# Attention scores on one core: the kernel moved into one critical section with its own semaphores, and one weight load for two products

## The chip, the core and the metric

One NeuronCore of a Trainium2 chip runs the kernel. The metric is the device time of one execution in microseconds (us), lower is better. Where I speak of a trace, it is of one execution, profiled; where I speak of a median, it is of 3 to 11 executions. PSUM is the memory that TensorE writes its products to, an eviction is the copy out of it, a store is the transfer of one head's result to memory, and a transfer lands when it reports itself done (each of the 16 DMA engines reports for its share).

## The reference

```python
def setup_inputs():
    batch, n_heads, seq, head_dim = 8, 12, 1024, 64
    return {"q": randn(batch, n_heads, seq, head_dim).astype(float32) * 0.1,
            "k": randn(batch, n_heads, seq, head_dim).astype(float32) * 0.1}

def reference(q, k):
    return np.einsum('bhid,bhjd->bhij', q, k).astype(np.float32)
```

There are 96 heads. Each takes two inputs of 1024x64 floats and gives 1024x1024 floats: 50.33 MB are read and 402.65 MB written. A head's result is 4.194 MB.

## The kernel before

The heads are worked in blocks of 2G heads, with G = 1, 1, 2, and then 4 eleven times. So block 0 is heads 0 and 1, block 1 heads 2 and 3, block 2 heads 4 to 7, block 3 heads 8 to 15, and so on. For each block the inputs are loaded, cast to half precision on GpSimd, transposed so that the head dimension lies on the partitions, multiplied on TensorE, copied out of PSUM by ScalarE and stored. A framework of tile pools places the semaphores.

```python
sizes = [1, 1, 2] + [GMAX] * (BH // (2 * GMAX) - 1)
PE_BLOCKS = 2                      # blocks 0 and 1 are transposed by TensorE
in_pool   = tile_pool(bufs=3)      # float32 inputs
half_pool = tile_pool(bufs=3)      # half-precision parts, two to a block
tr_pool   = tile_pool(bufs=2)      # transposed q and k of a block
out_pool  = tile_pool(bufs=3)      # one head's result, 32 KB a partition
po_pool   = tile_pool(bufs=2, space=PSUM)

def transpose_rows(self, x):       # blocks 0 and 1
    for t in range(NT):
        nc.tensor.transpose(t_ps[:, t], self.halves[x][:, t], ident)
    nc.vector.tensor_copy(out=dst, in_=src)

def transpose_quads(self, part, x):  # all others, 32x32 blocks
    nc.vector.transpose(out=dst, in_=src)

def scores(self, n, side):
    for u in range(NT // 2):
        for tt in range(2):
            for j in range(2):
                nc.tensor.matmul(ps[:, tt, js], qT[cs, g, 2*u + tt], kT[cs, g, js])
        nc.scalar.copy(out=dst, in_=ps)      # head 0: half of it on VectorE
        for do in side.get(u, []): do()      # transposes of the next block, loads
    nc.sync.dma_start(out=of[self.first + n]..., in_=o_sb...)
# ... (the first output buffer holds the inputs of blocks 0 to 2 at the start)
```

## Time and profile before

| | before |
|---|---|
| median of 3, first rounds | 1064.69 us (1064.45 to 1066.07) |
| traced execution | 1067.61 us, span 1065.8 |
| bytes moved | 453.26 MB |
| mean rate over the span | 425 GB/s |
| busiest compute engine | TensorE, 66% |

The DMA engines are full from 2 us to 1055 us, and no compute engine comes near to its limit.

### The profile page before, as it was taken

To read this page: it belongs to the slowest core of one execution; us is meant where nothing else is said; L and a number is where in the kernel's file an instruction comes from. 1 tells how busy PE (TensorE), PEld (TensorE's weight loads), DVE (VectorE), ACT (ScalarE), POOL (GpSimd) and SP (SyncE) were. 2 spreads that over 40 slices of the span, in tenths; PEclk is the share of its full clock that TensorE was granted. 3 is DMA by queue.
4 is the path that set the end of the run, shared out by engine and by line. 5 is a ranking of instruction groups with operands and counts; after the bars stand their busy time and mean duration, and the time that the engine had idled before them with its cause. 6 is when DMAs were issued, how large, how long until landed. Compare 5 with 4: busy or idle time off the path is not lost.

```text
span 1065.8 us, 4231 instructions
## 1 busy us (share of the span) xinstructions
PE 700.8 (66%) x1568; PEld 240.7 (23%) x1568; DVE 428.6 (40%) x57; ACT 694.3 (65%) x384; POOL 354.0 (33%) x206
## 2 busy tenths in 40 slices
PE   6686756756765675675675667567567667777770
PEld 2232212212222221221222222122122222222220
DVE  4768922900940670290094067029109406700000
ACT  2687657656765765666675677576667657777771
POOL 7769055036206505502620650550261064000000
DMA  9999999999999999999999999999999999999997
GB/s 384 440 430 434 421 427 439 427 429 427 434 422 433 433 431 421 435 427 424 434 433 413 433 431 418 422 434 423 426 432 432 428 430 432 432 433 433 432 430 313
DMA packets 21909, 453.26 MB, mean 425 GB/s; under 512 B 2432, under 2 KB 2432, under 8 KB 3968
## 3 DMA queue, kind: packets, MB, share of 16 engines
q1 hardware_dynamic: 14976, 406.85, 89.2%
q10 hardware_dynamic: 6912, 46.14, 10.4%
q8 instruction: 12, 0.20, 0.1%
q14 instruction: 9, 0.07, 0.0%
HBM read 50.33 MB, written 402.65 MB: 425 GB/s over the span
## 4 chain that ended last, share of the span: by engine, by line
DMA 70%; ACT 17%; PE 7%; DVE 1%; POOL 1%; issue 1%; ACTq 0%; SPq 0%; POOLq 0%
DMA out_dram<-o_sb 70%; ACT o_sb L166 17%; PE ps L155 7%; POOL half_sb L111 1%; DVE kT L128 0%; DMA early<-in_q_dram 0%; DVE o_sb L162 0%; DVE kT L139 0%; DVE o_sb L164 0%; PE ps L136 0%; ACT o_sb L161 0%; DVE qT L139 0%; ACTq L166 0%; POOL half_sb L93 0%; SPq L74 0%
## 5 line engine op out<-in xcount | busy, mean ns | idle before, releaser
L155 PE MATMUL ps<-kT,qT 64*128 64x512 f16 x1536 | 696.9, 617 | 333.6 <-ACT o_sb L166 328.2
L166 ACT COPY o_sb<-ps 128x2048 f32<-128x2048 f32 x379 | 689.0, 1868 | 335.5 <-DMA out_dram<-o_sb 302.2
L111 POOL CAST half_sb<-x_sb 32x2048 f16<-32x2048 f32 x176 | 332.1, 1887 | 531.6 <-DMA x_sb<-in_k_dram 507.1
L155 PEld LDWEIGHTS <-qT 64*128 64x128 f16 x1536 | 237.4, 157 | 791.2 <-issue 788.3
L128 DVE STREAM_TRANSPOSE qT<-half_sb 128x2048 f16<-128x2048 f16 (+1 forms) x24 | 214.2, 8926 | 477.8 <-POOL half_sb L111 477.8
L128 DVE STREAM_TRANSPOSE kT<-half_sb 128x2048 f16<-128x2048 f16 (+1 forms) x24 | 216.2, 9009 | 0.0
L111 POOL CAST half_sb<-early 32x1024 f16<-32x1024 f32 x16 | 16.5, 1033 | 2.6 <-DMA early<-in_k_dram 1.9
L136 PE MATMUL ps<-ident,half_sb 128*128 128x128 f16 x32 | 3.9, 309 | 6.7 <-POOL half_sb L93 6.2
L161 ACT COPY o_sb<-ps 128x1024 f32<-128x1024 f32 x4 | 4.0, 1012 | 5.5 <-PE ps L155 5.5
L162 DVE COPY o_sb<-ps 128x1024 f32<-128x1024 f32 x4 | 4.9, 1224 | 5.2 <-ACT o_sb L161 5.2
L161 ACT ACT_TABLE_LOAD x1 | 1.3, 1283 | 7.7 <-DMA early<-in_k_dram 7.7
L93 POOL CAST half_sb<-early 128x512 f16<-128x512 f32 x8 | 4.7, 613 | 3.4 <-DMA early<-in_q_dram 3.2
L139 DVE COPY qT<-ps 128x1024 f16<-128x1024 f16 x2 | 2.4, 1219 | 7.3 <-PE ps L136 7.3
L136 PEld LDWEIGHTS <-half_sb 128*128 128x128 f16 x32 | 3.3, 142 | 8.3 <-POOL half_sb L93 6.2
L139 DVE COPY kT<-ps 128x1024 f16<-128x1024 f16 x2 | 2.4, 1218 | 3.8 <-PE ps L136 3.8
L164 DVE COPY o_sb<-ps 128x2048 f32<-128x2048 f32 x1 | 2.3, 2292 | 2.0 <-PE ps L155 2.0
masks.py:199 POOL TENSOR_SCALAR_AFFINE_SELECT ident<-ident 128x128 f16<-128x128 f16 x1 | 0.3, 292 | 0.1
masks.py:197 POOL MEMSET ident<- 128x128 f16 x1 | 0.2, 204 | 0.3 <-POOLq L275 0.3
L275 POOL MEMSET const-float32-0.0<- 128x1 f32 x1 | 0.1, 98 | 0.2 <-issue 0.2
L275 POOL MEMSET const-bfloat16-1.0<- 128x1 bf16 x1 | 0.1, 100 | 0.0
L275 POOL MEMSET const-uint8-127<- 128x1 uint8 x1 | 0.1, 100 | 0.0
L275 POOL MEMSET const-float32-1.0<- 128x1 f32 x1 | 0.1, 98 | 0.0
## 6 DMA issues: line engine op xcount, KB each, us to landing
out_dram<-o_sb SPq DMA_DIRECT2D x96, 4096.0 KB, 23.2
x_sb<-in_k_dram ACTq DMA_DIRECT2D x22, 1024.0 KB, 29.6
x_sb<-in_q_dram ACTq DMA_DIRECT2D x20, 1024.0 KB, 18.6
x_sb<-in_q_dram SPq DMA_DIRECT2D x2, 1024.0 KB, 13.0
early<-in_k_dram ACTq DMA_DIRECT2D x4, 256.0 KB, 5.1
early<-in_q_dram SPq DMA_DIRECT2D x4, 256.0 KB, 4.7
early<-in_q_dram SPq DMA_DIRECT2D x2, 512.0 KB, 7.2
early<-in_k_dram ACTq DMA_DIRECT2D x2, 512.0 KB, 7.6
```

The source lines that it names most:

```text
L93: nc.gpsimd.tensor_copy(out=self.halves[x][:, :, half], in_=self.raw[half][:, x].rearrange("p (r d) -> p r d", d=D),)
L111: nc.gpsimd.tensor_copy(out=dst[:, :, b % 2], in_=raw[32 * b : 32 * b + 32, :, :, h],)
L128: pin(nc.vector.transpose(out=dst, in_=src))
L136: pin(nc.tensor.transpose(t_ps[:, t], self.halves[x][:, t], ident))
L139: pin(nc.vector.tensor_copy(out=dst, in_=src))
L155: nc.tensor.matmul(ps[:, tt, js], qT[cs, g, 2 * u + tt], kT[cs, g, js])
L161: pin(nc.scalar.copy(out=dst[:, 0], in_=ps[:, 0]))
L162: pin(nc.vector.tensor_copy(out=dst[:, 1], in_=ps[:, 1]))
L164: pin(nc.vector.tensor_copy(out=dst, in_=ps))
L166: pin(nc.scalar.copy(out=dst, in_=ps))
L275: nc = _bacc.Bacc("TRN2", target_bir_lowering=False, num_devices=1)
```

## The change

The intent is to spare the framework's waits and instructions. Everything stands in one critical section, each engine's order is written out by hand, and 18 semaphores replace the framework's. Two products that use the same q weights share one weight load. Along with it more changes: blocks 0 and 1 are now transposed by VectorE too, block 0's casts are shared out over three engines, head 1's evictions all go to ScalarE, some early loads are issued at other heads, and VectorE's order is fixed. The half-precision parts rotate through three buffers as before, but blocks 0 and 1 now take two each. The core of the diff, cut:

```diff
-    PE_BLOCKS = 2
-    half_pool = ctx.enter_context(tc.tile_pool(name="half_pool", bufs=3))
+    parts = [sb([P, 2 * GMAX * NT * D], F16, f"part{i}") for i in range(3)]
+        b.parts = [parts[(2 * i + p) % 3][:, : 2 * b.elems] for p in range(2)]
 ...
-                pin(nc.tensor.transpose(t_ps[:, t], self.halves[x][:, t], ident))
 ...
+    def pool_casts(b):
+        for half in range(2):
+            if half == 0:
+                if b.i == 1:
+                    nc.gpsimd.wait_ge(s_tr, 2)
+                elif b.i > 1:
+                    nc.gpsimd.wait_ge(s_tr, 4 * (b.i - 1) + 2)
+            nc.gpsimd.wait_ge(*b.loaded[half])
+            for dst, src in casts(b, half):
+                nc.gpsimd.tensor_copy(out=dst, in_=src).then_inc(s_cast, 1)
 ...
+                a = nc.tensor.matmul(o[:, t, :512], w, kT[cs, g, :512])
+                a = same_weights(a.ins, o[:, t, 512:], w, kT[cs, g, 512:])
 ...
+    with tc.tile_critical():
 ...
+        for n in range(4):
+            load(*stream.pop(0), (nc.sync, nc.scalar)[n % 2])
 ...
+        transposes(blocks[0])
+        for h in range(BH):
+            copies(h)      # head 2 waits for the last cast of block 2
+            store(h)
+            if h == 0:
+                for b in blocks[1:]:
+                    transposes(b)
```

## The prediction

> **What bounds the kernel now.** I read the page first: its slices, its chain of waits, its groups. Then the windows, the groups kept apart by form, and the timelines of the first 135 us.
>
> From the page (40 slices of 26.6 us; DMA is the mean busy share of the 16 DMA engines in tenths) and its chain:
>
> ```profile
> DMA  9999999999999999999999999999999999999997
> GB/s 384 440 430 434 421 427 439 427 429 427 434 422 433 433 431 421 435 427 424 434 433 413 433 431 418 422 434 423 426 432 432 428 430 432 432 433 433 432 430 313
> DMA 70%; ACT 17%; PE 7%; DVE 1%; POOL 1%; issue 1%; ACTq 0%; SPq 0%; POOLq 0%
> ```
>
> The DMA engines are full in every slice but the last; no compute engine passes 66%. The reader should see that there is no free time to win in the middle: 453.26 MB (402.65 of them the result) have to pass, and they pass at about 430 GB/s from the start.
>
> The windows (us, busy us and count by engine, granted clock, DMA share, GB/s) show how little is lost at the ends:
>
> ```profile
> 0.00:26.00 26.00, 15.53 (x53) 7.01 (x54) 10.67 (x8) 7.22 (x7) 19.51 (x28) 1.00 0.98 391
> 26.00:50.00 24.00, 17.17 (x44) 5.97 (x43) 18.77 (x5) 14.51 (x8) 16.78 (x11) 1.00 1.00 428
> 50.00:100.00 50.00, 38.05 (x84) 12.91 (x84) 36.31 (x4) 40.00 (x22) 38.42 (x21) 1.00 1.00 430
> 100.00:135.00 35.00, 23.70 (x53) 8.02 (x52) 31.07 (x4) 21.82 (x12) 7.59 (x5) 1.00 1.01 431
> 135.00:1000.00 865.00, 575.15 (x1268) 196.41 (x1268) 331.74 (x37) 577.82 (x318) 271.69 (x144) 1.00 1.00 429
> 1055.00:1066.00 11.00, 0.00 (x0) 0.00 (x0) 0.00 (x0) 0.00 (x0) 0.00 (x0) 1.00 0.31 135
> ```
>
> At the start only about 2.5 us are lost (26 us at 391 instead of 430). In the last 11 us the DMA engines end one after the other: the trace's landings of the last stores lie 8.6 us apart between the first and the last of the 16 engines, against 0.3 us for the first store and 1.8 us at 130 us. So some engines are slower, and the slowest sets the end. So the only thing a change of waits and instructions can do is to keep the DMA engines fed sooner, or to let them starve. It is the start that has to be followed, and for it I need durations:
>
> ```profile
> L166 ACT COPY o_sb<-ps 128x2048 f32<-128x2048 f32 x379 | 689.0, 1868 | 335.5 <-DMA out_dram<-o_sb 302.2 <-PE ps L155 25.4 <-POOL half_sb L111 7.6
> L128 DVE STREAM_TRANSPOSE qT<-half_sb 128x1024 f16<-128x1024 f16 x2 | 9.3, 4635 | 0.0
> L93 POOL CAST half_sb<-early 128x512 f16<-128x512 f32 x8 | 4.7, 613 | 3.4 <-DMA early<-in_q_dram 3.2
> L161 ACT COPY o_sb<-ps 128x1024 f32<-128x1024 f32 x4 | 4.0, 1012 | 5.5 <-PE ps L155 5.5
> L161 ACT ACT_TABLE_LOAD x1 | 1.3, 1283 | 7.7 <-DMA early<-in_k_dram 7.7
> ```
> ```profile
> 11.31 17.20 POOL L111 CAST half_sb<-early 32x1024 f16<-32x1024 f32 x16 [1.95 <-DMA early<-in_k_dram]
> 39.18 30.89 POOL L111 CAST half_sb<-x_sb 32x2048 f16<-32x2048 f32 x16 [6.40 <-DVE kT L128]
> 62.34 9.23 DVE L128 STREAM_TRANSPOSE qT<-half_sb 128x2048 f16<-128x2048 f16 x1 [14.63 <-POOL half_sb L111]
> 89.14 9.52 DVE L128 STREAM_TRANSPOSE kT<-half_sb 128x2048 f16<-128x2048 f16 x1
> 9.69 3.56 PE L155 MATMUL ps<-kT,qT 64*128 64x512 f16 x8 [1.59 <-DVE kT L139]
> 19.80 10.17 SPq L170 DMA_DIRECT2D out_dram<-o_sb  x2
> ```
>
> In these timelines (start, length, what): the 16 casts of block 2 take 17.2 us, of a block of four 30.9; four large transposes run from 62.34 to 98.66, so 36.3 us; the first product is at 9.69 and the first store at 19.80, while the loads still fill the DMA engines.
>
> **What the Trainium skill says.** "DMA: Bandwidth & Descriptors", section "Where 436 GB/s comes from", gives 435.2 GB/s as the ceiling of the path to SBUF; the trace agrees (429 to 433 when full). "TensorE: Matmul & The Clock Gate", section "Architectural detail: the array is 16× 32×32, not 1× 128×128", says TensorE can pull a weight load ahead of matmuls in flight; here matmuls with a 157 ns load between each start 0.43 us apart, which is that same page's cold gap of N/1.2 for N = 512 (section "Back-to-back issue gap"), so the load is hidden already. "VectorE: DVE Perf Modes", section "The three transpose paths", has the vector transpose at 32x32 blocks only, TensorE's whole; here eight TensorE transposes took 1.05 us and a 1.22 us copy, where a 128x1024 vector transpose takes 4.6.
>
> **The change, part by part.**
> (1) Shared weights: 768 of 1536 weight loads go. They are hidden, TensorE waits 328 us for evictions, and the DMA engines set the end: 0 us.
> (2) Own semaphores: fewer waits on the issuing queues. Loads are no longer held for a landing, but they already saturate the DMA engines: 0, at most 1 us.
> (3) Blocks 0 and 1 lose the TensorE transposes and go by vector transposes. Block 0: its loads land as before, 4.4 us (first half) and 5.7 us (second; block 0's last cast input). ScalarE issues 8 loads of 0.43 us from 0.73, to 4.2, loads its table to 5.5, then does 6 of the 16 casts. 512 columns by the line through 1.012 and 1.868 us are 0.58, say 0.6: to 9.1. VectorE (6) and GpSimd (4 of about 0.6) are done sooner. Four transposes of 512 columns: the step between starts is 4.33 us for 1024 and 8.93 for 2048, so about 2.15: to 17.8. Head 0: 16 matmuls at 0.43 and the last copy (VectorE, 1.22, now beside ScalarE's rather than after it) 8.3: first store at 26.1 instead of 19.8.
> (4) VectorE's order is now fixed: block 0, head 0's copies, then blocks 1, 2, 3. GpSimd's casts of block i+1 wait for the first two of block i's four transposes, as three part buffers serve two blocks. So the start is one serial chain: 26.1; first two transposes of block 1, 4.4: 30.5; casts of block 2, 17.2: 47.7; first two transposes of block 2, 9.1 (39.18 less 30.08): 56.8; casts of block 3, 30.9: 87.7; its transposes, 36.3: 124.0; head 8's first products 1.9 and four copies 7.5: store 8 is issued at 133.4. A first DMA flows about 1.5 us after its issue (windows of 2 us: 17 GB/s to 2 us, 315 after): 134.9.
> Before that store the DMA engines can only be given the loads of blocks 0 to 4 (12.58 MB) and 8 stores of 4.194 MB: 46.1 MB. The kernel before has moved 26x391 + 24x428 + 50x430 + 34.9x431 = 57.0 MB by then. The 10.9 MB short cost 10.9/0.429 = 25.3 us. As cross-check, the gaps: loads (8.39 MB) end at 22.5, store 0 flows at 27.6: 5 us. Stores 0 and 1 end near 47; store 2 has its copies held by the casts of block 2 (its buffer holds the early inputs) to 47.7, plus 7.6 and 1.5: 10 us. Stores 2 to 7 and four loads, 29.4 MB, fill 56.8 to 125; store 8 flows at 134.9: 10 us. The sum is 25. The slow DMA engines are behind by 1.8 us and use part of the gap: 25.3 - 1.8 = 23.5. After head 8, a block needs 30.9 of casts and 36.3 of transposes in some 88 us of DMA: hidden.
> Sum: 1064.7 + 23.5 = 1088.2.
>
> **Rivals.**
> A. The start is fed well enough and the DMA engines hide all: 1063 to 1066. For: the chain of before also has casts and transposes at the start, and an eviction stall of 7.6 us there cost nothing. Against: in before head 8's operands were ready at 98.7, in this at 124, and only three output buffers can lie ahead.
> B. Compute is quicker than I think at small sizes (512-column transposes, ScalarE casts): each microsecond of steps up to 26.1 moves the end by one; 4 us less gives 1084. If only the gap before store 8 vanished: about 1079.
> C. ScalarE, in order, also stands still for the load of block 4's third part, which waits for casts of block 3 (63 to 72 us); if this collides with stores being late, a further gap of some 5 us opens: 1093.
> D. The gain intended: fewer instructions and semaphores let the end come earlier, 1060. Against: the DMA engines at 429 GB/s have no room.
>
> **Range and chances.** The steps from 47.7 on are measured rows, good to some 2 us in sum; those before are estimates, good to 3; the lag of the slow engines and the tail to 2. Together about 4.5 us: 1081 to 1095 for 8 in 10. The line of 2% is 1086.0, half a deviation below my time. Faster by over 2%: 0.01, within 2%: 0.30, slower: 0.69.
>
> **What would show it.** First product near 17.8 us and first store near 26; ScalarE idle before head 2 until about 48 on GpSimd's casts; head 8's first product near 124 on VectorE's transpose; GB/s of the first five slices roughly 310, 310, 395, 430, 265, then 430 as before; weight loads 768; matmuls still 0.43 us apart. It is wrong if the DMA share stays at 9 in the first five slices, if the middle runs at another rate than 429, or if the spread of the engines at the end differs much from 8.6 us.

## The result, and the profile after

| | before | changed |
|---|---|---|
| median, same rounds | 1065.42 us (1064.45 to 1068.12, 6 runs) | 1095.45 us (1090.94 to 1099.89, 6 runs) |
| ratio | | 1.0281 (1.0249 to 1.0314) |
| traced execution | 1067.61 us | 1092.85 us |

A ratio is the mean time of one kernel's runs over that of the other's of the same rounds, so it is not quite the ratio of the medians. The changed kernel is slower, by 30.0 us in the median. The prediction was 1088.2 us with a range to 1095.0: the direction held, and the size fell 0.45 us outside the range.

The DMA rates of the changed kernel, from the page (40 slices, 27.3 us each), and its chain of waits:

```profile
GB/s 308 308 378 429 271 419 440 429 432 431 435 427 426 439 430 431 429 434 432 427 431 427 426 438 420 427 438 430 425 427 434 420 426 435 431 431 436 426 435 298
DMA 64%; ACT 16%; PE 7%; DVE 6%; POOL 4%; issue 1%; ACTq 0%; DVEq 0%; POOLq 0%; SPq 0%
```

Slices 1, 2, 3 and 5 run far below 430, and from the sixth on the row looks as before. VectorE and GpSimd have entered the chain with 6% and 4% where they had 1% each. The windows of the changed kernel give the same stretches as those shown of before:

```profile
0.00:26.00 26.00, 6.71 (x16) 1.24 (x8) 16.63 (x13) 8.01 (x10) 12.84 (x24) 1.00 0.81 323
26.00:50.00 24.00, 10.97 (x25) 1.86 (x12) 10.56 (x6) 8.48 (x6) 16.53 (x16) 1.00 0.81 350
50.00:100.00 50.00, 36.90 (x80) 6.12 (x40) 27.44 (x6) 37.54 (x21) 30.19 (x16) 1.00 0.87 362
100.00:135.00 35.00, 12.11 (x27) 2.16 (x14) 26.04 (x3) 12.54 (x8) 25.95 (x14) 1.00 0.75 323
135.00:1000.00 865.00, 591.28 (x1283) 97.59 (x641) 361.27 (x40) 582.37 (x321) 275.92 (x147) 1.00 1.00 429
```

The second last number of a line is the DMA share. It was 0.98 or more in all of these stretches before, and is 0.75 to 0.87 up to 135 us now. In the long stretch after that it is 1.00 at 429 GB/s in both. The two later gaps are seen by themselves in narrow windows: the share is 0.05 from 47 to 57 us and 0.21 from 125 to 137, and 0.91 or more between them.

Why the DMA engines stand still is read from the timelines of GpSimd, VectorE and ScalarE in the changed kernel (start, length, what; in brackets the idle time before and what ended it):

```profile
14.76 10.61 POOL L138 CAST part<-out 32x512 f16<-32x512 f32 x16 [7.13 <-DVE tr0k L155]
32.34 17.43 POOL L138 CAST part<-out 32x1024 f16<-32x1024 f32 x16 [6.97 <-DVE tr1k L155]
58.83 31.09 POOL L138 CAST part<-in 32x2048 f16<-32x2048 f32 x16 [9.06 <-DVE tr0k L155]
...
49.88 4.55 DVE L155 STREAM_TRANSPOSE tr0q<-part 128x1024 f16<-128x1024 f16 x1 [13.07 <-POOL part L138]
90.02 9.21 DVE L155 STREAM_TRANSPOSE tr1q<-part 128x2048 f16<-128x2048 f16 x1 [22.56 <-POOL part L138]
...
49.80 3.63 ACT L213 COPY out<-ps 128x2048 f32<-128x2048 f32 x2 [14.31 <-POOL part L138]
128.12 3.63 ACT L213 COPY out<-ps 128x2048 f32<-128x2048 f32 x2 [21.97 <-PE ps L160]
```

The two engines take turns: GpSimd waits for the first two of a block's four transposes before it casts the next block, then VectorE waits for these casts. Only the last two transposes of a block run beside the casts of the next. ScalarE waits 14.31 us before head 2 for the last cast of block 2, whose inputs lie in its output buffer, and 21.97 us before head 8 for its products. The eviction that store 8 waits for, in the kernel before and in the changed one (each line is the last two of head 8's four copies):

```profile
96.36 3.63 ACT L166 COPY o_sb<-ps 128x2048 f32<-128x2048 f32 x2 [0.18 <-PE ps L155]
132.00 3.64 ACT L213 COPY out<-ps 128x2048 f32<-128x2048 f32 x2 [0.25 <-PE ps L160]
```

So store 8 was issued at 100.0 us in the kernel before and at 135.7 in the changed one. The steps on the path, predicted and traced (ends, us):

| step | predicted | traced |
|---|---|---|
| casts of block 0 | 9.1 | 10.0 |
| transposes of block 0 | 17.8 | 19.2 |
| store 0 issued | 26.1 | 27.7 |
| casts of block 2 | 47.7 | 49.8 |
| first two transposes of block 2 | 56.8 | 58.8 |
| casts of block 3 | 87.7 | 89.9 |
| transposes of block 3 | 124.0 | 126.0 |
| store 8 issued | 133.4 | 135.7 |

Where the 30 us went is best counted from the trace's DMA packets. I take the time at which 60 MB had been moved, and the time from there to the landing of the last store. The first number takes in the whole start; the second is 393 MB of steady work.

| trace | 60 MB moved at | from there to the last landing |
|---|---|---|
| before, 1067.61 us | 143.1 | 921.4 |
| changed, 1092.85 us | 169.5 | 920.2 |

So the start lost 26.4 us. At 137.2 us, when the changed kernel's store 8 begins to flow, it had moved 46.2 MB and the kernel before 57.5. The traced execution of before was its slow one by 2.2 us and the traced one of the changed kernel was fast by 2.6; so in the median some 3.5 us more come from the second part. The experiments were made to show whether the first is what I think it is, and what the second is.

### The profile page after: what moved, and what is told of

Its sections match the earlier page's. It is cut to its first block, busy times and chain, and to the rows that moved or that the text cites. A ratio compares the mean times of both kernels' runs of the same rounds, so it can differ in the third digit from the quotient of the medians.

```text
span 1091.0 us, 3320 instructions
## 1 busy us (share of the span) xinstructions
PE 707.8 (65%) x1536; PEld 117.0 (11%) x768; DVE 441.9 (41%) x66; ACT 699.8 (64%) x391; POOL 361.4 (33%) x216
## 4 chain that ended last, share of the span: by engine, by line
DMA 64%; ACT 16%; PE 7%; DVE 6%; POOL 4%; issue 1%; ACTq 0%; DVEq 0%; POOLq 0%; SPq 0%
DMA out_dram<-out 64%; ACT out L213 16%; POOL part L138 4%; PE ps L191 4%; PE ps L160 3%; DVE tr1q L155 2%; DVE tr1k L155 2%; DVE tr0q L155 1%; DVE tr0k L155 1%; ACTq L111 0%; ACT part L240 0%; ACT L240 0%; DVE out L209 0%; ACTq L204 0%; DVEq L146 0%
## 5 line engine op out<-in xcount | busy, mean ns | idle before, releaser
L213 ACT COPY out<-ps 128x2048 f32<-128x2048 f32 x380 | 690.8, 1868 | 349.9 <-DMA out_dram<-out 277.7
L138 POOL CAST part<-in 32x2048 f16<-32x2048 f32 x176 | 332.1, 1887 | 539.3 <-DMA in<-in_k_dram 502.6
L191 PE MATMUL ps<-tr1k,tr1q 64*128 64x512 f16 x400 | 254.5, 636 | 187.9 <-ACT out L213 162.8
L191 PE MATMUL ps<-tr0k,tr0q 64*128 64x512 f16 x368 | 234.0, 636 | 170.5 <-ACT out L213 147.0
L160 PE MATMUL ps<-tr1k,tr1q 64*128 64x512 f16 x400 | 251.4, 629 | 0.0
L160 PE MATMUL ps<-tr0k,tr0q 64*128 64x512 f16 x368 | 231.3, 629 | 0.0
L155 DVE STREAM_TRANSPOSE tr1q<-part 128x2048 f16<-128x2048 f16 (+1 forms) x14 | 116.5, 8318 | 275.7 <-POOL part L138 275.7
L155 DVE STREAM_TRANSPOSE tr0q<-part 128x2048 f16<-128x2048 f16 (+2 forms) x14 | 107.2, 7656 | 231.7 <-POOL part L138 230.1
L155 DVE STREAM_TRANSPOSE tr1k<-part 128x2048 f16<-128x2048 f16 (+1 forms) x14 | 117.5, 8390 | 0.0
L191 PEld LDWEIGHTS ps<-tr1k,tr1q 64*128 64x128 f16 x400 | 61.0, 152 | 495.9 <-ACT out L213 396.8
L155 DVE STREAM_TRANSPOSE tr0k<-part 128x2048 f16<-128x2048 f16 (+2 forms) x14 | 108.1, 7724 | 0.0
L191 PEld LDWEIGHTS ps<-tr0k,tr0q 64*128 64x128 f16 x368 | 56.1, 152 | 451.9 <-ACT out L213 356.3
L208 ACT COPY out<-ps 128x1024 f32<-128x1024 f32 x4 | 4.0, 1012 | 13.4 <-PE ps L160 13.4
## 6 DMA issues: line engine op xcount, KB each, us to landing
in<-in_q_dram SPq DMA_DIRECT2D x2, 1024.0 KB, 17.8
out<-in_q_dram SPq DMA_DIRECT2D x2, 512.0 KB, 10.5
```

The lines of the kernel that those rows point to most:

```text
L138: nc.gpsimd.tensor_copy(out=dst, in_=src).then_inc(s_cast, 1)
L155: nc.vector.transpose(out=dst, in_=src).then_inc(s_tr, 1)
L160: return pe.add_instruction(mybir.InstMatmult(name=nc.get_next_instruction_name(), engine=before.engine, ins=[pe.lower_ap(rhs), pe.lower_a ...
L191: a = nc.tensor.matmul(o[:, t, :512], w, kT[cs, g, :512])
L208: nc.scalar.copy(out=dst[:, 0], in_=ps[e % 2][:, 0]).then_inc(s_cp, 1)
L213: nc.scalar.copy(out=dst, in_=ps[e % 2]).then_inc(s_cp, 1)
```

## The experiments

The theories, by the letters that the expectations use. S: the start is one serial chain, and the loss is set by when store 8 is issued, since until then the DMA engines can be given only 46.1 MB. M: something in the middle or at the end of the run costs what the start does not explain. W: the shared weight load costs something itself. G: each gap of the DMA engines costs its own length. Q: the DMA engines drift apart because two queues alternate. R: a starved start makes the rest slower too. All runs gave correct results.

### The changed kernel again, unedited

> The changed kernel without an edit, for a second trace and six or so more times. Theory S (a serial chain at the start: the loss is set when store 8, the store of head 8, is issued): 1090 to 1100 us again, store 8 issued near 135.7 us, five first slices as in the first trace. Theory M (something in the middle or at the end costs the 5 us by which the median lies above the traced run of 1092.85): if this trace is of a slower execution, its chain to store 8 is the same within 1 us and the extra time shows as a lower rate between 135 and 1000 us or as a longer tail.

Measured: 1096.25 us median (1095.51 to 1097.01, 4 runs), ratio 1.0291 (1.0276 to 1.0307). The trace is of an execution of 1097.01 us, 4.2 us slower than the first. Store 8 was issued at 135.8 us and 60 MB were moved at 169.7, both as in the first trace; from there to the last landing it took 924.2 us, where the first took 920.2. So the start is the same in each execution to 0.2 us, and the scatter of the changed kernel lies in the rest. That part of M holds.

### Every product with its own weight load

```diff
-                a = same_weights(a.ins, o[:, t, 512:], w, kT[cs, g, 512:])
+                a = nc.tensor.matmul(o[:, t, 512:], w, kT[cs, g, 512:])
```

> Only the shared weight load undone: every product loads its own weights, 1536 loads. Theory S: the same as the changed kernel within 0.3%, for loads are hidden and the DMA engines set the end. Rival W (the shared load itself costs: the first weight load of a group now stands behind the wait for the eviction, a head of evictions takes 7.82 us where it took 7.66): 3 us or more faster.

Measured: 1096.65 us median (1093.39 to 1100.41, 4 runs), ratio 1.0296. That is the same as the unedited kernel, as S has it, and W falls. The groups of weight loads in this run (idle time before them at the end of the line) show something that I had wrong in W:

```profile
L192 PEld LDWEIGHTS ps<-tr1k,tr1q 64*128 64x128 f16 x400 | 65.1, 163 | 53.4 <-issue 53.4
L191 PEld LDWEIGHTS ps<-tr1k,tr1q 64*128 64x128 f16 x400 | 60.7, 152 | 402.7 <-ACT out L213 321.5 <-issue 55.1 <-DVE tr1k L155 26.2
```

The weight load at the head of a group waits for ScalarE's eviction here as well, although nothing is shared. It is the hand-written wait, which stands in front of the load, and not the sharing, that keeps it from being done ahead. It makes each pair of evictions wait 0.25 to 0.31 us instead of 0.18 to 0.22. The versions with packed parts below have the same waits and take no longer than the kernel before once 60 MB are moved, so it costs nothing that these runs can show.

### Packed parts: the casts of blocks 1 and 2 wait for no transpose

The small blocks need little room: the parts of blocks 0 and 1 fill exactly one buffer and those of block 2 another. The kernel before also kept blocks 0 and 1 in one buffer.

```diff
-        b.parts = [parts[(2 * i + p) % 3][:, : 2 * b.elems] for p in range(2)]
+        if i < EARLY:
+            home, off = parts[i // 2], (i % 2) * 4 * b.elems
+            b.parts = [home[:, off + p*2*b.elems : off + (p+1)*2*b.elems] for p in range(2)]
+        else:
+            b.parts = [parts[(2 * (i - EARLY) + 2 + p) % 3] for p in range(2)]
 ...
-                if b.i == 1:
-                    nc.gpsimd.wait_ge(s_tr, 2)
-                elif b.i > 1:
+                if b.i == EARLY:
+                    nc.gpsimd.wait_ge(s_tr, 8)
+                elif b.i > EARLY:
                     nc.gpsimd.wait_ge(s_tr, 4 * (b.i - 1) + 2)
```

> Only the place of the half-precision parts changed: blocks 0 and 1 share the first part buffer, block 2 has the second, so that the casts of blocks 1 and 2 wait for no transpose and those of block 3 for block 1's. Same memory, instructions and order. Theory S: casts of block 2 end near 36 us, of block 3 near 68, store 8 is issued near 116 instead of 135.7; the two later gaps go (20 us of 26.7), the first of 6.7 us stays: 1071 us (1068 to 1076). Theory M: only the part of the loss that lies in the start can go, and 5 us stay on top: 1076 or more, with the same scatter of 9 us.

Measured: 1073.22 us median (1070.56 to 1077.39, 4 runs), ratio 1.0088 (1.0061 to 1.0115), which is 23.0 us less than the changed kernel of the same rounds. GpSimd's timeline and the page's rates of this run:

```profile
7.91 28.27 POOL L145 CAST part<-out 32x512 f16<-32x512 f32 x32
37.02 31.09 POOL L145 CAST part<-in 32x2048 f16<-32x2048 f32 x16 [0.83 <-DVE tr1k L162]
```
```profile
GB/s 314 373 433 433 430 432 434 432 430 426 434 430 427 431 431 429 434 437 421 438 431 434 420 439 427 428 432 425 434 431 432 424 436 431 434 433 432 430 432 331
```

GpSimd now casts blocks 1 and 2 without a pause, beside VectorE, and goes on with block 3 at 37.02 us instead of 58.83. Store 8 was issued at 113.9 us (116 expected) and 60 MB were moved at 150.6. The later gaps are gone, and the first stays in the first two slices. No instruction was removed and no wait of the steady part was touched, so what cost these 23 us was the early reuse of a part buffer. Of the start, 7.5 us stay lost (60 MB at 150.6 against 143.1). They go with the first store, at 27.8 us against 19.8; no run gives block 0 its TensorE transposes back, so that these are the whole reason is not shown by an experiment.

### Two more loads at the start

```diff
-        for n in range(4):
+        for n in range(6):
             load(*stream.pop(0), (nc.sync, nc.scalar)[n % 2])
 ...
-            for _ in range({2: 2, 3: 1, 4: 1}.get(h % 8, 0)):
+            for _ in range({2: 0 if h == 2 else 2, 3: 1, 4: 1}.get(h % 8, 0)):
```

> Two more loads (2.1 MB, 4.9 us of DMA) at the start, into the free third input buffer, instead of after head 2. Theory S: they fill most of the first gap, but what can be given to the DMA engines before store 8 stays 46.1 MB, and store 8 is issued at the same time: no gain (within 1 us), the later gaps grow by what the first loses. Rival G (each gap costs what it is long, and filling one saves it): 4 to 5 us faster than the changed kernel of the same rounds.

Measured: 1095.99 us median (1094.86 to 1098.65, 4 runs), ratio 1.0292, the same as the unedited kernel. The page's rates:

```profile
GB/s 370 318 344 420 231 416 439 427 430 430 436 430 426 437 434 419 439 424 430 426 433 420 424 425 411 430 433 430 411 426 437 417 428 427 434 431 434 426 435 284
```

The first slice rose from 308 to 370, and the third and fifth fell from 378 and 271 to 344 and 231. Filling one gap only made the later ones longer, so G falls. Store 8 was issued 1.0 us later than in the first trace, at 136.7, as ScalarE had one more load to issue ahead of its casts, and 60 MB were moved 1.0 us later, at 170.5.

### Packed parts and the two loads together

The edit is the two above in one.

> The packed parts and the two earlier loads together. Theory S: now store 8 is no longer late, so filling the first gap counts: of the 6.9 us that the packed parts alone lose at the start some 4 to 5 go, against the packed parts alone 1073.2: 1068 to 1070 us. If each part adds up only as alone (the two loads gained 0 on the changed kernel), 1073 again.

Measured: 1072.01 us median (1068.06 to 1073.98, 4 runs), ratio 1.0053 (1.0028 to 1.0078). 60 MB were moved at 148.5 us instead of 150.6: of the 4 to 5 us hoped for, 2.1 came at the start. The reason is S itself, which I had not applied far enough: store 8 was issued at 114.7, and with two loads done sooner the DMA engines had again nothing to do just before it (396 GB/s between 100 and 135 us). The time alone (1.2 us under the packed parts, of other rounds) does not tell the two expectations apart; the 60 MB do.

### The later loads on the stores' queue

```diff
-                    load(*stream.pop(0), nc.scalar)
+                    load(*stream.pop(0), nc.sync)
```

> As the run with packed parts and six early loads, but the 40 later loads are issued on the stores' queue (SyncE) instead of ScalarE's, so that one queue holds all. Theory Q (the engines drift apart because loads and stores of two queues alternate on each DMA engine): in the blocks with loads the slowest engine needs 87.3 us as the fastest instead of 88 to 89, the spread at the end falls below 4 us from 7 to 11, and the time falls by 5 to 8 us, to about 1062. Rival: the drift belongs to the engines or to reading, whatever the queue: same time within 2 us, spread at the end 7 us or more.

Measured: 1079.24 us median (1077.15 to 1080.41, 4 runs), ratio 1.0124: 7 us slower than the run above instead of 5 to 8 us faster. 60 MB were moved at 148.4 us, as there, but the rest took 927.1 us. The landings of the last store lay 9.8 us apart. Q falls. In this kernel it was of use that the loads stood on another queue than the stores. Why is not shown: a load's wait for its buffer now also stands in front of the stores behind it in the queue, and no run separates this from the sharing of the queue.

### The kernel before, again

> The kernel before, unchanged, for a second trace of it. If the middle of the run differs between the kernels (theory M), its blocks with loads are paced below 88.5 us by the slowest engine and the whole from 60 MB moved to the end below 921 us; if the extra 3 us of the changed kernel are the scatter of the drift alone, this stretch lies between 917 and 927 us as in the five traces of the changed kernel and its variants.

Measured: 1065.38 us median (1064.78 to 1065.92, 4 runs), ratio to itself 0.9996. The trace, of an execution of 1065.02 us, has 60 MB moved at 142.9 us and 919.0 us from there to the last landing. With the first trace this gives what the rest takes in the kernel before: 919.0 and 921.4. The expectation of M (below 921 in a trace near the median) holds, and its 88.5 us a block too: from head 15 to head 79 the last landings came every 88.1 us here. The other reading's range, 917 to 927, holds as well, so this run alone did not decide.

### Every store in two halves

```diff
-        nc.sync.wait_ge(s_cp, 4 * h + 4)
-        nc.sync.dma_start(out=of[h]..., in_=outs[(h + 1) % 3]...).then_inc(s_out[(h + 1) % 3], 16)
+        for v in range(2):
+            nc.sync.wait_ge(s_cp, 4 * h + 2 * v + 2)
+            ts = slice(4 * v, 4 * v + 4)
+            nc.sync.dma_start(out=of[h]...[:, ts], in_=outs[(h + 1) % 3][:, ts]
+            ).then_inc(s_out[(h + 1) % 3][v], 16)
```

(On top of the packed parts and the six loads; ScalarE waits for each half of an output buffer by itself.)

> As the run with packed parts and six early loads, but each head is stored in two halves of 2 MB as soon as two of its four copies are done, and each half of an output buffer comes free by itself. Theory S: the first store is issued 3.4 us sooner (about 25 instead of 28.7), which closes what is left of the first gap: 2 to 3 us faster than that run, about 1066. Rival: twice the number of transfers costs at each of 192 stores: slower.

Measured: 1071.96 us median (1071.53 to 1072.65, 4 runs), ratio 1.0056, the same as with whole stores. The start gained what was expected (first store at 25.1 us; 60 MB at 145.0 instead of 148.5), and the rest lost it again: 924.4 us, at 427 GB/s between 135 and 1000 us instead of 430 (the 430 is of the fastest execution of the kernel with whole stores). That the stores themselves are dearer is seen in the landings: from head 15 to head 47 the first of the 16 DMA engines to land needed 88.1 us for eight heads in the mean, where it needs 87.4 in the other traces as long as the engines lie within 7 us of one another. The rival is right about the middle, S about the start.

### A gap planted before head 8

```diff
             nc.tensor.wait_ge(s_tr, 4 * (b.i + 1))
+            if b.i == EARLY:
+                nc.tensor.wait_ge(s_cast, cast_done(EARLY + 1, 1))
```

> As the run with packed parts and six early loads (median 1072.0, traced: 60 MB moved at 148.5 us, 916.3 us from there to the last landing), but head 8's products also wait for the last cast of block 4, which comes some 14 us later than their own operands: a gap planted late in an otherwise fed start. Theory S (a late store 8 costs what the DMA engines then stand still): store 8 issued near 128 instead of 114.7, 60 MB moved near 160 to 162, time 1083 to 1086. Rival R (a start that starves also makes the rest slower, by letting all DMA engines begin again in step: in the changed kernel the stretch after 60 MB is 3 to 4 us longer by the medians): another 3 to 4 us, 1087 or more.

Measured: 1088.64 us median (1083.63 to 1092.87, 6 runs), ratio 1.0216 (1.0192 to 1.0241, so whether it is 2% slower is unclear). TensorE's timeline at head 8 and the rates of this run:

```profile
118.52 0.62 PE L200 MATMUL ps<-tr1k,tr1q 64*128 64x512 f16 x1 [26.70 <-POOL part L145]
```
```profile
GB/s 378 417 406 436 186 412 426 441 433 424 433 432 422 439 430 426 426 435 427 430 435 431 430 433 428 424 430 439 431 421 439 426 423 432 437 431 430 437 429 313
```

Store 8 was issued at 128.1 us as expected, and 60 MB were moved at 161.9, so the gap cost 13.4 us by itself: that is S, shown by putting the loss in rather than taking it out. The median is 16.6 us above the one without the gap, which was run in other rounds: 3 more than the gap, and inside what R expected. So is the scatter: 9 us here and 9 us in the changed kernel, against 4 in the first six runs of before. By the intervals of the two ratios the 16.6 us is good to some 4 us only, so the run alone does not prove the 3.

### Head 0 alone in two halves

```diff
+        if h == 0:
+            for v in range(2):
+                nc.sync.wait_ge(s_cp, 2 * v + 2)
+                nc.sync.wait_ge(s_cp0, 2 * v + 2)
+                ts = slice(4 * v, 4 * v + 4)
+                nc.sync.dma_start(out=of[h]...[:, ts], in_=outs[1][:, ts]).then_inc(s_out[1], 16)
+            return
```

> As the run with packed parts and six early loads, with head 0 alone stored in two halves, the first some 3.4 us sooner, all other stores whole. Theory S: the first gap closes as in the run with half stores (60 MB moved at 145 to 146 us instead of 148.5) without that run's slower middle (924 us): 1068 to 1070. Rival: the rest varies by as much as this gains: 1072 again.

Measured: 1075.86 us median (1074.14 to 1078.97, 5 runs), ratio 1.0106. The expectation was wrong: the first store was issued at 24.7 us, but 60 MB were moved at 148.1, as without the halves. Head 8's store came at 114.3 as before, and the gap that was closed in front had opened there (375 GB/s in the fifth slice). It is the third time that earlier work gained little because store 8 had not moved. The rest took 923.5 us, which fits the rival.

### Packed parts again, unedited

> The kernel with packed parts unchanged, for a second trace and more times, since its first trace was of its fastest execution. Theory R: its rest after 60 MB stays at 916 to 920 us in the median (time 1071 to 1073). If the 3 to 4 us are scatter that any of these kernels shows: rest 920 to 924, time up to 1077.

Measured: 1073.23 us median (1069.82 to 1076.24, 6 runs), ratio 1.0074. The trace, of an execution of 1073.51 us, has 60 MB at 150.5 us and 919.8 us after that. The first trace had 916.8 in the fastest execution of its rounds. Theory R's expectation holds for the rest; the time is 0.2 us above its range.

### What the runs say together

For S, the issue of head 8's store against the time at which 60 MB were moved, over seven traces:

| kernel | store 8 issued | 60 MB moved at | both, less those of the changed kernel |
|---|---|---|---|
| changed | 135.7 | 169.5 | 0, 0 |
| two more loads | 136.7 | 170.5 | +1.0, +1.0 |
| planted gap | 128.1 | 161.9 | -7.6, -7.6 |
| packed, six loads | 114.7 | 148.5 | -21.0, -21.0 |
| head 0 in halves | 114.3 | 148.1 | -21.4, -21.4 |
| all stores in halves (first half of store 8) | 110.8 | 145.0 | -24.9, -24.5 |
| packed parts alone | 113.9 | 150.6 | -21.8, -18.9 |

In all but the last the two move together to within 0.4 us. The last had its loads later and lost some 3 us more in the first gap.

For the rest, the traces must be set right for being of faster or slower executions. The start hardly differs between executions (169.5, 169.7 and 169.9 us in three traces of the changed kernel and the one with its own weight loads), so I add to each trace's rest the median time of its kernel less the time of the traced execution:

| kernel | rest in the trace | set to the median |
|---|---|---|
| before, two traces | 921.4, 919.0 | 919.2, 919.4 |
| packed parts, two traces | 916.8, 919.8 | 919.5, 919.5 |
| packed, six loads | 916.3 | 920.3 |
| changed, two traces | 920.2, 924.2 | 922.8, 923.4 |
| own weight loads | 927.4 | 923.6 |
| two more loads | 925.0 | 922.3 |
| planted gap | 918.6 | 923.6 |
| head 0 in halves | 923.5 | 924.6 |
| all stores in halves | 924.4 | 923.7 |
| loads on the stores' queue | 927.1 | 927.6 |

The four kernels that starved longest at the start (changed, own weights, two more loads, planted gap) lie at 922.3 to 923.6, and before and the two packed kernels with whole stores at 919.2 to 920.3. So R describes these, with medians of 4 to 6 executions that scatter by up to 9 us. It does not describe the halves and the stores' queue, which starve little and are slow as well.

What is common to most of the slow ones is seen in the landings of the stores, block by block of eight heads from head 15 to head 79. In the blocks that begin with the last of the 16 DMA engines less than 7 us behind the first, the first needs 87.2 to 87.8 us (55 blocks of twelve traces, all but the one with half stores; 87.4 in the mean). In those that begin with 9 us or more between them it needs 87.7 to 90.8 (21 blocks, 88.7 in the mean). The last one needs 88.0 us a block in one trace of the packed parts and 89.4 in that of the own weight loads. I read this as the three output buffers no longer bridging the difference. By an estimate from the issues and landings of the stores and 1.5 us from an issue to its first bytes, the first engines ran dry after head 8 for some 6 us in all in the trace of the own weight loads and in the second of the changed kernel, 2.5 with two more loads, and 0 to 0.4 in both traces of before, the first of the changed kernel, the packed parts (with and without the six loads) and the planted gap. It is not a clear border: the first trace of before also had 9.2 to 10.4 us between its engines from head 39 to head 63. The run with all stores in halves is slow in another way: its engines lie only 5.3 us apart at the end, and all of them are slower. Why the slow engines fall behind more in one kernel or execution than in another stays open. The trace's packets do not name their engine, and the one trial that aimed at a cause, the loads on the stores' queue, made it worse.

None of the versions beat the kernel before. The best, packed parts with six early loads (with whole stores or with halves, 1072.01 and 1071.96 us), is 0.5% slower than it, and 2% faster than the changed kernel.

## Why the prediction was right or wrong

**Shared weights, 0 us.** Right, and shown by undoing it: 1096.65 against 1096.25 us. That the load is hidden is shown too, by the starts of the products in the changed kernel: 19.73, 20.16 and 20.59 us, 0.43 apart whether a load stands between them or not. The prediction inferred it from the 0.43 us being the page's cold gap. The number agrees, but the granted clock was 1.0 in every window, so that the array was cold is not shown.

**Own semaphores, 0 to 1 us.** No run takes them out alone. The packed kernel with six loads has them all and has a rest of 920.3 us where before has 919.3, so no gain in the steady part is seen.

**The vector transposes of block 0.** Right in kind, 1.6 us too short at the first store: the four transposes of 512 columns took 9.2 us together, where the prediction had 8.7, and ScalarE's casts ended 0.9 us later, having waited for its own load issues and its table.

**The serial chain.** Right step by step, from the first store to the issue of store 8: 108.0 us traced, 107.3 predicted. It was shown as the cause by taking the buffer reuse away (23.0 us less), by planting a gap (13.4 us more at the start), and by the two loads that gained nothing. The cross-check by three gaps was right in their sum but would have misled: a gap that is filled comes back before store 8.

**25.3 us for the missing bytes.** This is the first term that was mis-sized, by little: 26.4 us measured. Two errors partly cancelled: store 8 came 2.3 us later than predicted, which is 1.0 MB, and the kernel before had moved 56.6 MB at 134.9 us instead of 57.0.

**"The slow DMA engines are behind by 1.8 us and use part of the gap: 25.3 - 1.8 = 23.5."** This is the step that failed. I took the drift of the engines for a reserve that a gap would give back. The gap did bring them together: the stores of heads 8 to 11 landed within 0.2 to 0.4 us on all 16 engines in the two traces of the changed kernel, and within 1.8 to 3.5 in those of before. But this was not kept: at the last store the engines of the changed kernel lay 9.1 and 10.5 us apart, those of before 8.6 and 9.1. In the median the stretch after 60 MB did not get shorter, it became longer by some 3.5 us (922.8 and 923.4 against 919.2 and 919.4). So the term has the other sign: 26.4 + 3.5 is 29.9, and 30.0 were measured. What makes the 3.5 us stays open, as said above. The single trace of the first rounds would have hidden this (1091.0 less 1065.8 is a span of 25.2 us more), as it was a fast execution of one kernel against a slow one of the other.

**What would show it.** The slices came out as 308, 308, 378, 429 and 271 GB/s against 310, 310, 395, 430 and 265; the first product at 19.3 us, head 8's at 126.1; 768 weight loads; matmuls 0.43 us apart; 429 GB/s in the middle and a last spread of 9.1 us.

**The range.** I gave the tail and the engines' lag 2 us. The changed kernel's executions alone scatter over 9, and its two traces put it after the start. The range ended 0.45 us too low.

**The rivals.** A and D fell at once. B was wrong in sign, as the small sizes were slower than thought. C came true as a stall (ScalarE stood 9.65 us before head 4 for a cast, to 74.8 us) but opened no further gap: the DMA share was 1.02 from 59 to 75 us and 0.95 from 75 to 85, as the engines had stores 2 and 3 to do.

## What to carry to other kernels

Where the DMA engines are full, count the bytes that they can have been given before each store and find the store that comes too late: only its time counts, and filling a gap before it gained 0 to 2 us here. When buffers are handed out anew, check the first few small blocks by themselves, because a rotation that suits the steady state can turn two engines that worked side by side into two that take turns. And before the last few microseconds of a difference are explained by one trace, ask where in its kernel's scatter that execution lay.

## What the Trainium skill lacked or had wrong

- "DMA: Bandwidth & Descriptors", section "Latency and other measured facts", has engines 7 and 15 as usually slower and ties it, as a best guess, to descriptors made by GpSimd. Here all transfers of the program came from the SyncE and ScalarE queues, and the engines drifted apart all the same: the last store of before landed on ten of the 16 at 1056.0 to 1057.7 us and on six at 1062.6 to 1064.5 in its first trace, and on seven at 1052.9 to 1053.7 and nine at 1058.0 to 1062.0 in its second. Which engines these are the traces do not say.
- No page has such a drift among the engines over a run: in the first trace of before it grew from 0.4 us at the first store to 10.4 at head 55, in blocks with loads beside the stores (the last engine needed 87.5 to 89.6 us for one, the first 87.2 to 88.7). In the two last blocks, of stores alone, both needed 77.4 to 77.8 and it stayed at 8.5 to 8.6.
- No page gives a price for halving a store that is already large, in a queue that is kept full: with 192 stores of 2 MB instead of 96 of 4 MB the first engine to land needed 88.1 us for eight heads (head 15 to 47, in the mean) instead of 87.4.
- "VectorE: DVE Perf Modes", section "The three transpose paths", has 311 ns for 128x128 of bf16 on VectorE. The 128x512 transposes of fp16 here, with a strided result, took 2.54 to 2.67 us in the mean of each tile, which is 635 to 668 ns for 128 columns. Whether the stride makes the difference no run shows.
